# Two of the eight weight chunks of each gate and up product: the low part by an accumulating transfer in place of a VectorE subtraction

## The chip, the cores and the metric

The kernel runs on one core of one Trainium2 chip. Its engines are TensorE (PE: matrix products into PSUM; PEld is its weight load), VectorE (DVE), ScalarE (ACT), GpSimd (POOL) and SyncE (SP, which here issues the weight transfers). Each runs its own instructions in order and waits on semaphores for the others. The metric is the time of the program on the device in microseconds; a median of three runs is shown.

## What is computed

The reference is one layer of a decoder for 256 tokens of 2048 features: a combined input projection, sliding-window attention and a Mamba-2 mixer side by side, a gated merge, a feed-forward part, a per-layer embedding and a final norm. The part that matters here:

```
f = rmsnorm(h, g_ffn[i])                                            # h: 256 x 2048
h = h + (jax.nn.silu(f @ w_gate[i]) * (f @ w_up[i])) @ w_down[i]    # w_gate, w_up: 2048 x 5632
```

All weights and activations are float32.

## The kernel before

Each product is made of three TensorE products of rounded operands. A float32 matrix is split into a high part (the value rounded to float32r, a type that TensorE takes at full pace) and a low part (what the rounding left), and a product is hi*hi + hi*lo + lo*hi, summed in PSUM. The activations lie transposed in SBUF, split once (`hT` for the feed-forward part). The weights are streamed and split as they come.

`nblock` makes one block of 512 output columns. It goes through the 2048 input features in chunks of `kc` = 2 tiles of 128, so in eight chunks. For a chunk, SP's queue loads the weights, 128 partitions x 2 x 512 float32 or 512 KB, into `wr` (L181); ScalarE writes the high part `wh` (L188); VectorE writes the low part `wl` = `wr` - `wh` (L190). Then TensorE runs twelve matmuls: for each of the two feature tiles and the two token tiles one of L199 (`wh` under the high activations), one of L200 (`wl` under the high activations), and one of L201 (`wh` under the low activations). The first matmul of a chunk needs only `wh`; the second already needs `wl`.

The buffers come from pools that go round: four slots for `wr`, four for `wh`, three for `wl`. So `wl` of a chunk goes into the slot of the chunk three before, and its writer must wait until TensorE has read that one. The order of instructions on each engine is fixed when the program is built; semaphores do the rest.

The feed-forward part is in `hidden` (L834). For each of eleven column blocks j it calls `nblock` for the gate, then for the up product. The gate goes through ScalarE's Silu (L838), the two are multiplied on VectorE (L842), and the transposes of the result (L145) are put between the first chunks of the next gate block by `pump`. The blocks come in two halves, j = 0 to 5 and 6 to 10, each followed by the down product (L866). That is 22 gate and up blocks, 176 chunks. In this part GpSimd has next to nothing to do: it computes r3 at the start, and issues the transfers of `pt` and `gfin` (L861, L864) in the second half.

Of the kernel before, what the change touches and what calls it, by code (L numbers as in the profile page):

```python
# [18 lines left out]
P = 128  # L19
# [4 lines left out]
NB = 512  # L24
# [37 lines left out]
def block_kernel(ctx: ExitStack, tc: tile.TileContext, x, x_t, p_t, positions, vecs, rows, g_final,  # L62
# [25 lines left out]

    # work that runs beside the streaming products, a step per weight chunk from each queue
    side, heads = deque(), deque()  # L90
# [14 lines left out]

# [1 line left out]
    ident = const.tile([P, P], F32, name="ident")  # L107
# [6 lines left out]

# [1 line left out]
    def bcast_mid(ap, n):  # L116
# [7 lines left out]
    def split_to(dst, j0, ps, gains=None):  # L124
        """ps [128, 2, 256]: two transposed feature tiles, into the hi and lo parts of dst."""
        if gains is None:
            nc.scalar.copy(out=dst[:, 0, j0:j0 + 2, :], in_=ps)
            nc.vector.tensor_tensor(out=dst[:, 1, j0:j0 + 2, :], in0=ps,
                                    in1=dst[:, 0, j0:j0 + 2, :].bitcast(F32), op=ALU.subtract)
        else:  # L130
            for j in range(2):
                nc.scalar.activation(out=dst[:, 0, j0 + j, :], in_=ps[:, j, :], func=AF.Copy,
                                     scale=gains[j])
                nc.vector.scalar_tensor_tensor(out=dst[:, 1, j0 + j, :], in0=ps[:, j, :],  # L134
                                               scalar=gains[j],
                                               in1=dst[:, 0, j0 + j, :].bitcast(F32),
                                               op0=ALU.mult, op1=ALU.subtract)

    def transpose_pair(src, col0, dst, j0, gains=None):
        """Columns col0..col0+255 of the two token tiles, transposed, into dst[:, :, j0:j0+2]."""  # L140
        ps = aux_tile().rearrange("p (j t) -> p j t", j=2)
        for j in range(2):
            for t in range(NT):
                c = col0 + j * P
                nc.tensor.transpose(out=ps[:, j, t * P:(t + 1) * P], in_=src[t][:, c:c + P],  # L145
                                    identity=ident)
        split_to(dst, j0, ps, gains)
# [7 lines left out]
    def mean_parts(n, eps, name):  # L155
        """Partial means of squares per token tile, and eps beside them."""
        m = const.tile([P, NT, n + 1], F32, name=name)
        nc.vector.memset(m[:, :, n:n + 1], eps)
        return m
# [4 lines left out]
    def rsqrt_mean(parts, out_r):  # L164
        """parts [128, n, m] of mean_parts -> out_r [128, n]."""
        n = out_r.shape[1]
        s = stat_p.tile([P, NT], F32, name="rms_s")[:, :n]
        nc.vector.tensor_reduce(out=s, in_=parts, op=ALU.add, axis=AX.X)  # L168
        nc.gpsimd.tensor_tensor(out=out_r, in0=s, in1=mhalf[:, :n], op=ALU.pow)  # L169

    def nblock(w, col0, lhs, nk, subs=((0, NB),), pumps=1, before=None, kc=2):
        """Columns of w against transposed activations: hi*hi + hi*lo + lo*hi.

        Returns, per sub-block of columns, the two token tiles in PSUM."""
        width = sum(s[1] for s in subs)
        accs = [[acc_tile() for _ in range(NT)] for _ in subs]
        for c in range(nk // kc):
            if before is not None:
                before(c)
            wr = wraw_p.tile([P, kc, width], F32, name="wr", tag="wr")  # L180
            nc.sync.dma_start(  # L181
                out=wr, in_=w[c * kc * P:(c + 1) * kc * P, col0:col0 + width].rearrange(
                    "(k p) n -> p k n", p=P))
            wh = whi_p.tile([P, kc, width], F32R, name="wh", tag="wh")
# [4 lines left out]
            wl = wlo_p.tile([P, kc, width], F32R, name="wl", tag="wl")  # L189
            nc.vector.tensor_tensor(out=wl, in0=wr, in1=wh.bitcast(F32), op=ALU.subtract)  # L190
            for kk in range(kc):
# [13 lines left out]

# [1 line left out]
    warm = roll("warm")  # L207
# [14 lines left out]

    # 1 where column >= row; 1 where row > column
    upper = const.tile([P, P], F32, name="upper")
# [8 lines left out]
    nc.vector.tensor_copy(out=below_r, in_=below)  # L233
    # additive window mask over the previous and the own key block
    amask = const.tile([P, 2 * P], F32, name="amask")
# [27 lines left out]

    # pairs of feature tiles, ahead of the weights that meet them
    split_at = {0: 0, 1: 1, 3: 2, 5: 3, 7: 4, 9: 5, 10: 6, 11: 7}
# [24 lines left out]

# [1 line left out]
    def evac_rows(ps, width, col0, dst, r):  # L292
# [4 lines left out]
    def conv_pair(src, col0, ctile, acc):  # L297
        """Two channel tiles: transpose, causal depthwise convolution; into acc [128, 2, 256]."""
        ps = aux_tile().rearrange("p (j t) -> p j t", j=2)
# [37 lines left out]

    # B block, with the transposes of x ahead of the chunks that need them
    accs = nblock(w_in, BO, lhs_u, KD, pumps=0, before=load_u, kc=1)
# [3 lines left out]

    # angles of the rotary embedding, reduced to [-pi, pi]
    rot = const.tile([P, NT, 2, HD // 2], F32, name="rot")

    def make_rot():
        pos_f = stat_p.tile([P, NT], F32, name="pos_f")
        nc.vector.tensor_copy(out=pos_f, in_=pos_i)
        # the angle of |position|; the sine takes the sign back  # L350
        sgn = stat_p.tile([P, NT], F32, name="pos_sgn")
# [32 lines left out]
        for c in (c1, c2, c3, c4):  # L384
            less(k, c)
        # cosine as the sine a quarter turn on
        nc.vector.tensor_scalar(out=kh, in0=ang, scalar1=float(np.pi / 2), scalar2=None,
# [16 lines left out]

    # C block and dt
    W2 = (NB + SSM_H) // 2
# [20 lines left out]
    def make_dt():  # L427
# [5 lines left out]
        nc.scalar.activation(out=e, in_=e, func=AF.Exp)  # L433
        # log(1 + e) = 2 atanh(e / (2 + e))
        s = t3("dt_s")
# [39 lines left out]
    def queue_decay(g):  # L475
        """Decay matrices of group g, one token chunk after the other, times C B^T."""
        builds, products = [], []
# [112 lines left out]

# [1 line left out]
    # heads h and h + 4 of each eight side by side, as their key heads lie in kT  # L592
    qrot = big([P, NT, NH, HD], F32, name="qrot")
    kk = big([P, 2, NKV * SEQ], F32, name="kk")
    krot = kk[:, 0, :NT * NKV * HD].rearrange("p (t h d) -> p t h d", t=NT, h=NKV)
    kT = kk[:, 1].rearrange("p (h k) -> p h k", h=NKV)
    # values beside zeros, left for the even and right for the odd head of a feature tile
    vz = [big([P, NT, NKV, 2, 2, HD], F32R, name="vz") for _ in range(2)]
# [4 lines left out]
    def rope(ps, t, dst):  # L603
        """Four heads in PSUM columns; dst [128, 4, 64]."""
        pv = ps.rearrange("p (h a d) -> p h a d", h=4, a=2)
# [56 lines left out]
    def queue_heads(g):  # L662
# [46 lines left out]
        def p_flip():  # L709
            s = mix.pop(("s", g))  # L710
            # [keys, parity, pair, queries]: both query blocks on the first keys, one on the others
            pt = [big([P, 2, 2, 3 * P], F32R, name="pt") for _ in range(2)]
# [47 lines left out]

# [1 line left out]
    merged = [big([P, D], F32, name="merged") for _ in range(NT)]  # L762
# [45 lines left out]

# [1 line left out]
    h = [big([P, D], F32, name="h") for _ in range(NT)]  # L810
# [21 lines left out]

# [1 line left out]
    def hidden(j, dst):  # L834
        accs = nblock(w_gate, j * NB, lambda k: stat(hT, k), KD)
        act = [roll("act") for _ in range(NT)]
        for t in range(NT):
            nc.scalar.activation(out=act[t], in_=accs[0][t], func=AF.Silu,  # L838
                                 scale=r3[:, t:t + 1])
        accs = nblock(w_up, j * NB, lambda k: stat(hT, k), KD)  # L840
        for t in range(NT):
            nc.vector.scalar_tensor_tensor(out=act[t], in0=accs[0][t], scalar=r3[:, t:t + 1],  # L842
                                           in1=act[t], op0=ALU.mult, op1=ALU.mult)
        for i in range(2):
            side.append(lambda i=i: transpose_pair(act, i * 2 * P, dst, 2 * i))
# [31 lines left out]

# [1 line left out]
    ssq5 = mean_parts(5, EPS, "ssq5")  # L879
# [4 lines left out]
    def load_last(c):  # L884
        """Weights of the last block of columns, kept whole so that one token tile can end
        before the other."""
        wr = wraw_p.tile([P, 2, NB], F32, name="wr", tag="wr")
# [7 lines left out]
    def mix_in(t, ps, pp, c0, n):  # L895
        """h += sigmoid(gate) * proj on n columns from c0."""
        gt = roll("gt")[:, :n]
        hc = h[t][:, c0:c0 + n]
        nc.scalar.activation(out=gt, in_=ps, func=AF.Sigmoid, scale=r4[:, t:t + 1])
        nc.vector.tensor_tensor(out=gt, in0=gt, in1=pp, op=ALU.mult)  # L900
        nc.vector.tensor_tensor(out=hc, in0=hc, in1=gt, op=ALU.add)
# [120 lines left out]
```

## Time and profile before

| | |
|---|---|
| Median of 3 runs | 1625.88 us (1624.92 to 1626.29) |
| Span of the profiled execution | 1623.2 us |
| TensorE busy | 1600.3 us, 99% |
| VectorE busy | 915.8 us, 56% |
| ScalarE busy | 775.8 us, 48% |
| GpSimd busy | 142.1 us, 9% |
| Weight queue of SP | 290.75 MB, 58.6% of the 16 DMA engines |
| GpSimd's transfers | 3.47 MB, 0.6% |

The span is the time from the first to the last instruction of the one execution that was profiled, which is all that is known of that execution's own time; it is 2.7 us under the median of the runs. TensorE's matmuls are pipelined, and a matmul's length in the rows (0.39 us) overlaps with the next: the distance between two starts (0.23 us) is its cost.

### The profile page before, as it was taken

The numbers are of one execution on the slowest core, as the hardware profiler recorded it, in microseconds if no ns is written. First come the engines' busy times: TensorE is split into PE (matmuls) and PEld (weight loads), VectorE is DVE, ScalarE is ACT, GpSimd is POOL, SyncE is SP. The second block draws the span as 40 slices with busy tenths as digits, with TensorE's granted clock in tenths as the row PEclk, the third lists the DMA queues.
The fourth block names the chain that finished last, engine by engine and source line by source line (L and its number), as shares of the span: only waits on it lengthen the run. The fifth ranks groups of instructions, "written<-read, shape, count | busy, mean of one in ns | idle before, by whom it ended". The sixth has DMA issues, their size and how long they took to land.

```text
span 1623.2 us, 19872 instructions
## 1 busy us (share of the span) xinstructions
PE 1600.3 (99%) x7414; PEld 1326.0 (82%) x7414; DVE 915.8 (56%) x1062; ACT 775.8 (48%) x991; POOL 142.1 (9%) x144
## 2 busy tenths in 40 slices
PE   8999999999999999999999999999999999999997
PEld 6888888888888888888888888888888888888876
DVE  8777576665655555555555545444545454555673
ACT  6545665465543444445544444433344444454552
POOL 5023233313100000000000000000000000000000
PEclk9999999999999999999999999999999999999999
DMA  6765445555556666555666666556666676555671
GB/s 201 212 185 165 131 118 160 149 171 171 164 199 220 190 188 190 182 194 184 192 186 190 189 187 192 186 194 193 194 195 187 189 223 187 193 183 190 198 233 52
DMA packets 152433, 296.63 MB, mean 183 GB/s; under 512 B 9408, under 2 KB 9536, under 8 KB 151952
## 3 DMA queue, kind: packets, MB, share of 16 engines
q1 hardware_dynamic: 151040, 290.75, 58.6%
q0 software_dynamic: 576, 3.47, 0.6%
q8 instruction: 58, 0.95, 0.2%
q10 hardware_dynamic: 720, 1.14, 0.2%
q14 instruction: 39, 0.32, 0.1%
HBM read 293.23 MB, written 2.10 MB: 182 GB/s over the span
## 4 chain that ended last, share of the span: by engine, by line
PE 93%; DVE 2%; ACT 2%; DMA 1%; issue 1%; POOL 0%; POOLq 0%; ACTq 0%
PE acc L200 29%; PE acc L199 29%; PE acc L201 29%; PE aux L145 1%; DVE wl L190 1%; ACT sc L698 1%; PE aux L557 1%; DMA wr<-in_w_ple_gate_dram 1%; PE aux L734 1%; PE aux L496 0%; DMA wr<-in_w_in_dram 0%; ACT wh L188 0%; PE aux L303 0%; PE aux L718 0%; DVE uT L134 0%
## 5 line engine op out<-in xcount | busy, mean ns | idle before, releaser
L190 DVE TENSOR_TENSOR wl<-wr,wh 128x1024 fp32r<-128x1024 f32 (+2 forms) x556 | 687.0, 1239 | 568.6 <-PE acc L200 511.8
L188 ACT CAST wh<-wr 128x1024 fp32r<-128x1024 f32 (+2 forms) x555 | 570.6, 1030 | 710.8 <-PE acc L201 667.2
L199 PE MATMUL acc<-wh,uT 128*128 128x512 f32 (+1 forms) x704 | 277.0, 394 | 2.6 <-ACT cb L294 1.5
L200 PE MATMUL acc<-wl,uT 128*128 128x512 f32 (+1 forms) x704 | 270.4, 384 | 6.1 <-DVE wl L190 6.0
L199 PE MATMUL acc<-wh,hT 128*128 128x512 f32 x704 | 275.7, 392 | 0.0
L201 PE MATMUL acc<-wh,hT 128*128 128x512 f32 x704 | 274.2, 390 | 0.0
L200 PE MATMUL acc<-wl,hT 128*128 128x512 f32 x704 | 274.0, 389 | 0.0
L201 PE MATMUL acc<-wh,uT 128*128 128x512 f32 (+1 forms) x704 | 269.4, 383 | 0.0
L200 PEld LDWEIGHTS acc<-wl,uT 128*128 128x128 f32 x704 | 132.8, 189 | 35.4 <-DVE wl L190 10.8
L199 PEld LDWEIGHTS acc<-wh,uT 128*128 128x128 f32 x704 | 132.6, 189 | 28.2 <-ACT cb L294 1.7
L201 PEld LDWEIGHTS acc<-wh,hT 128*128 128x128 f32 x704 | 132.1, 188 | 27.7
L200 PEld LDWEIGHTS acc<-wl,hT 128*128 128x128 f32 x704 | 132.2, 188 | 26.9
L199 PEld LDWEIGHTS acc<-wh,hT 128*128 128x128 f32 x704 | 132.2, 188 | 26.8
L201 PEld LDWEIGHTS acc<-wh,uT 128*128 128x128 f32 x704 | 132.5, 188 | 25.3
L199 PE MATMUL acc<-wh,actT 128*128 128x512 f32 x352 | 137.6, 391 | 0.0
L201 PE MATMUL acc<-wh,actT 128*128 128x512 f32 x352 | 137.2, 390 | 0.0
L200 PE MATMUL acc<-wl,actT 128*128 128x512 f32 x352 | 137.2, 390 | 0.0
L201 PEld LDWEIGHTS acc<-wh,actT 128*128 128x128 f32 x352 | 66.1, 188 | 13.7
L199 PEld LDWEIGHTS acc<-wh,actT 128*128 128x128 f32 x352 | 66.1, 188 | 13.5
L200 PEld LDWEIGHTS acc<-wl,actT 128*128 128x128 f32 x352 | 66.1, 188 | 13.4
L169 POOL TENSOR_TENSOR r<-rms_s,mhalf 128x2 f32<-128x2 f32 (+1 forms) x6 | 4.4, 740 | 583.7 <-DVE rms_s L168 583.7
L199 PE MATMUL acc<-wh,mergedT 128*128 128x512 f32 x128 | 50.5, 394 | 0.0
(271 smaller groups left out, 1613.8 us busy)
## 6 DMA issues: line engine op xcount, KB each, us to landing
wr<-in_w_in_dram SPq DMA_DIRECT2D x152, 512.0 KB, 3.7
wr<-in_w_gate_dram SPq DMA_DIRECT2D x88, 512.0 KB, 3.7
wr<-in_w_up_dram SPq DMA_DIRECT2D x88, 512.0 KB, 3.7
wr<-in_w_down_dram SPq DMA_DIRECT2D x88, 512.0 KB, 3.6
wr<-in_w_ssd_br_dram SPq DMA_DIRECT2D x32, 512.0 KB, 4.2
wr<-in_w_o_dram SPq DMA_DIRECT2D x32, 512.0 KB, 4.3
wr<-in_w_ple_gate_dram SPq DMA_DIRECT2D x32, 512.0 KB, 4.6
wr<-in_w_attn_br_dram SPq DMA_DIRECT2D x16, 512.0 KB, 4.5
```

Source lines behind the costliest of these rows:

```text
L145: nc.tensor.transpose(out=ps[:, j, t * P:(t + 1) * P], in_=src[t][:, c:c + P], identity=ident)
L169: nc.gpsimd.tensor_tensor(out=out_r, in0=s, in1=mhalf[:, :n], op=ALU.pow)
L188: nc.scalar.copy(out=wh, in_=wr)
L190: nc.vector.tensor_tensor(out=wl, in0=wr, in1=wh.bitcast(F32), op=ALU.subtract)
L199: nc.tensor.matmul(o, hi[:, ts], wh[:, kk, cs], start=(k == 0), stop=False)
L200: nc.tensor.matmul(o, hi[:, ts], wl[:, kk, cs], start=False, stop=False)
L201: nc.tensor.matmul(o, lo[:, ts], wh[:, kk, cs], start=False, stop=(k == nk - 1))
L557: nc.tensor.matmul(ps[:, es], m[:, t, e, :], xd[:, t, 0, es], start=True, stop=True)
L698: nc.scalar.activation(out=s[:, h, ks], in_=s[:, h, ks], func=AF.Exp, bias=mx[:, t, h:h + 1], accum_out=den[:, t, h:h + 1])
L734: nc.tensor.matmul(ps[:, :, qs], vz[vi][:, kt, g, a].rearrange("p b d -> p (b d)"), pt[pi][:, a, :, cs], start=(kt == 0 and a == 0 and vi ...
```

## The change

In `nblock` the chunks whose numbers are in `added` get their low part in another way: ScalarE writes the negated, rounded weights into `wl`, and then a transfer issued from GpSimd's queue reads the same weights once more from HBM and adds them to what lies in `wl`. The sum is `wl` = w - round(w), as before. `hidden` passes `added=(3, 7)` for both products, so it is 2 of 8 chunks, 44 in all. The other products keep the subtraction. Removed comments and docstrings are left out of the diff here; they move the line numbers by up to six (L200 becomes L206).

```diff
-    def nblock(w, col0, lhs, nk, subs=((0, NB),), pumps=1, before=None, kc=2):
+    def nblock(w, col0, lhs, nk, subs=((0, NB),), pumps=1, before=None, kc=2,
+               added=()):
...
             wr = wraw_p.tile([P, kc, width], F32, name="wr", tag="wr")
-            nc.sync.dma_start(
-                out=wr, in_=w[c * kc * P:(c + 1) * kc * P, col0:col0 + width].rearrange(
-                    "(k p) n -> p k n", p=P))
+            wd = w[c * kc * P:(c + 1) * kc * P, col0:col0 + width].rearrange(
+                "(k p) n -> p k n", p=P)
+            nc.sync.dma_start(out=wr, in_=wd)
...
             wl = wlo_p.tile([P, kc, width], F32R, name="wl", tag="wl")
-            nc.vector.tensor_tensor(out=wl, in0=wr, in1=wh.bitcast(F32), op=ALU.subtract)
+            if c in added:
+                nc.scalar.activation(out=wl, in_=wr, func=AF.Copy, scale=-1.0)
+                nc.gpsimd.dma_start(out=wl, in_=wd, accum_op=ALU.add)
+            else:
+                nc.vector.tensor_tensor(out=wl, in0=wr, in1=wh.bitcast(F32), op=ALU.subtract)
...
-        accs = nblock(w_gate, j * NB, lambda k: stat(hT, k), KD)
+        accs = nblock(w_gate, j * NB, lambda k: stat(hT, k), KD, added=(3, 7))
...
-        accs = nblock(w_up, j * NB, lambda k: stat(hT, k), KD)
+        accs = nblock(w_up, j * NB, lambda k: stat(hT, k), KD, added=(3, 7))
```

What this does to the order on the engines is seen at the second gate block (j = 1). On ScalarE before, from the two Silu of the first gate (`act`) to the copies of the second block; the first five `wh` are chunks 3 to 7 of the up block, the next those of the gate block of j = 1 from its chunk 0, with `wh_6715` as chunk 3:

```order
L838 ACTIVATE act_6491<-acc_6345,r3_6337 128x512
L188 CAST wh_6552<-wr_6550 128x1024
L188 CAST wh_6570<-wr_6568 128x1024
L188 CAST wh_6588<-wr_6586 128x1024
L188 CAST wh_6606<-wr_6604 128x1024
L188 CAST wh_6624<-wr_6622 128x1024
L188 CAST wh_6647<-wr_6645 128x1024
L188 CAST wh_6672<-wr_6670 128x1024
L188 CAST wh_6697<-wr_6695 128x1024
L188 CAST wh_6715<-wr_6713 128x1024
L188 CAST wh_6733<-wr_6731 128x1024
L127 CAST actT_6343<-aux_6663 128x512
```

The end of the same stretch now, from chunk 7 of the up block (`wh_6627`) on; `wh_6719` is chunk 3 of the gate block:

```order
L190 CAST wh_6627<-wr_6625 128x1024
L193 ACTIVATE wl_6629<-wr_6625 128x1024
L190 CAST wh_6651<-wr_6649 128x1024
L190 CAST wh_6676<-wr_6674 128x1024
L190 CAST wh_6701<-wr_6699 128x1024
L190 CAST wh_6719<-wr_6717 128x1024
L193 ACTIVATE wl_6721<-wr_6717 128x1024
L127 CAST actT_6343<-aux_6667 128x512
L190 CAST wh_6738<-wr_6736 128x1024
```

The negating copy (L193) stands right behind its chunk's `wh` and ahead of the `wh` of the next chunk; the copy of the transposes (L127) has come ahead of chunk 4's `wh`.

On TensorE the matmuls stand in the same order as before; only what they wait for has changed. Before, at chunk 3 of that gate block, with the semaphore that each waits for:

```order
L201 MATMUL acc_6644<-wh_6697,hT_5652 128x512
L199 MATMUL acc_6643<-wh_6715,hT_5652 128x512 [waits Activation_49]
L200 MATMUL acc_6643<-wl_6717,hT_5652 128x512 [waits DVE_49]
L201 MATMUL acc_6643<-wh_6715,hT_5652 128x512
L199 MATMUL acc_6644<-wh_6715,hT_5652 128x512
L200 MATMUL acc_6644<-wl_6717,hT_5652 128x512
```

Now, at the same place:

```order
L207 MATMUL acc_6647<-wh_6701,hT_5652 128x512
L205 MATMUL acc_6648<-wh_6701,hT_5652 128x512
L206 MATMUL acc_6648<-wl_6703,hT_5652 128x512
L207 MATMUL acc_6648<-wh_6701,hT_5652 128x512
L205 MATMUL acc_6647<-wh_6719,hT_5652 128x512 [waits Activation_49]
L206 MATMUL acc_6647<-wl_6721,hT_5652 128x512 [waits DMASW0_49]
```

The second matmul of the chunk waited for VectorE and now waits for a transfer of GpSimd's queue (DMASW).

On GpSimd's queue nothing stood between `r3` and `pt` before. The end of the stage now, from the last gate block on:

```order
L194 DMA wl_10454<-in_w_gate_dram 128x2x512
L194 DMA wl_10527<-in_w_gate_dram 128x2x512
L867 DMA pt_10715<-in_p_t_dram 128x512
L194 DMA wl_10606<-in_w_up_dram 128x2x512
L194 DMA wl_10679<-in_w_up_dram 128x2x512
L870 DMA gfin_10719<-in_g_final_dram 128x2048
```

The 44 transfers (L194) stand one behind the other, and `pt` and `gfin` among the last of them.

## Rows read from the trace of the kernel before

**Rows 1.** The page's first part: span, then busy us, share, instructions

```profile
span 1623.2 us, 19872 instructions
...
PE 1600.3 (99%) x7414; PEld 1326.0 (82%) x7414; DVE 915.8 (56%) x1062; ACT 775.8 (48%) x991; POOL 142.1 (9%) x144
```

**Rows 2.** The page's slices: granted TensorE clock in tenths

```profile
PEclk9999999999999999999999999999999999999999
```

**Rows 3.** The page's costliest groups: busy us, mean ns, idle before and releaser

```profile
L190 DVE TENSOR_TENSOR wl<-wr,wh 128x1024 fp32r<-128x1024 f32 (+2 forms) x556 | 687.0, 1239 | 568.6 <-PE acc L200 511.8
...
L200 PE MATMUL acc<-wl,uT 128*128 128x512 f32 (+1 forms) x704 | 270.4, 384 | 6.1 <-DVE wl L190 6.0
```

**Rows 4.** Stretches: length; busy of PE, PEld, DVE, ACT, POOL; clock, DMA, GB/s

```profile
776.00:1045.00 269.00, 269.00 (x1215) 222.60 (x1214) 136.24 (x126) 118.95 (x129) 0.71 (x1) 1.00 0.65 190
...
1176.00:1396.00 220.00, 220.00 (x988) 182.12 (x987) 108.67 (x97) 93.50 (x97) 1.10 (x2) 1.00 0.66 196
```

**Rows 5.** Groups by line, 776 to 1396 us: busy us, mean ns, idle before

```profile
L190 DVE TENSOR_TENSOR wl<-wr,wh 128x1024 fp32r<-128x1024 f32 x224 | 274.3, 1224 | 284.6 <-PE acc L200 271.7 <-issue 9.2 <-ACT act L838 1.9
...
L188 ACT CAST wh<-wr 128x1024 fp32r<-128x1024 f32 x224 | 236.2, 1055 | 344.3 <-PE acc L201 341.2 <-DMA wr<-in_w_up_dram 1.9 <-issue 1.2
```

**Rows 6.** Timeline, 829.3 to 836 us: start, length, instruction, idle before it

```profile
829.34 0.39 PE L200 MATMUL acc<-wl,hT 128*128 128x512 f32 x1
...
829.76 1.23 DVE L190 TENSOR_TENSOR wl<-wr,wh 128x1024 fp32r<-128x1024 f32 x1 [0.69 <-PE acc L200]
...
829.99 1.06 ACT L188 CAST wh<-wr 128x1024 fp32r<-128x1024 f32 x1 [1.64 <-PE acc L201]
...
831.05 3.11 SPq L181 DMA_DIRECT2D wr<-in_w_up_dram  x2
...
835.23 0.39 PE L199 MATMUL acc<-wh,hT 128*128 128x512 f32 x1
...
835.46 0.39 PE L200 MATMUL acc<-wl,hT 128*128 128x512 f32 x1
```

**Rows 7.** Timeline of a gate block's start, 822.9 to 830.1 us

```profile
823.42 1.23 DVE L190 TENSOR_TENSOR wl<-wr,wh 128x1024 fp32r<-128x1024 f32 x1 [0.62 <-issue]
...
826.61 0.60 PE L145 MATMUL aux<-ident,act 128*128 128x128 f32 x4
...
830.02 0.39 PE L200 MATMUL acc<-wl,hT 128*128 128x512 f32 x1
```

**Rows 8.** DMA issues: out<-in, queue, count, KB each, median us to landing

```profile
wr<-in_w_gate_dram SPq DMA_DIRECT2D x88, 512.0 KB, 3.7
...
gfin<-in_g_final_dram POOLq DMA_DIRECT2D x1, 1024.0 KB, 7.5
...
pt<-in_p_t_dram POOLq DMA_DIRECT2D x1, 256.0 KB, 5.3
...
pos_i<-in_positions_dram POOLq DMA_DIRECT2D x1, 1.0 KB, 3.7
```

**Rows 9.** Line L812, the two h transfers: issues in ns, times to landing

```profile
L812 POOL DMA_DIRECT2D h<-in_x_dram x2: 530/568/605, 457.3 to 503.3; - x2
...
DMA to landing us min/median/max: 5.9/6.6/7.2
```

**Rows 10.** Timeline of TensorE, 1562 to 1572 us

```profile
1566.51 0.50 PE L199 MATMUL acc<-wh,h2T 128*128 128x512 f32 x1 [3.45 <-ACT gt L899]
...
1568.46 0.63 PE L199 MATMUL acc<-wh,h2T 128*128 128x512 f32 x1
1568.89 0.63 PE L200 MATMUL acc<-wl,h2T 128*128 128x512 f32 x1
...
1571.42 0.39 PE L200 MATMUL acc<-wl,h2T 128*128 128x512 f32 x1
```

**Rows 11.** Timeline of TensorE, 24 to 29 us

```profile
28.31 0.61 PE L200 MATMUL acc<-wl,uT 128*128 128x512 f32 x1 [2.33 <-DVE wl L190]
```

**Rows 12.** Stretch of 28 to 30 us, columns as in rows 4

```profile
28.00:30.00 2.00, 1.69 (x5) 1.30 (x5) 2.00 (x6) 0.00 (x0) 0.85 (x1) 0.64 0.31 70
```

## The prediction

> **What bounds the kernel now.** I read the page from the top: the span and the engines' shares, then the slices, then the costliest groups with the idle time ahead of them, and last the stage that is changed. TensorE is busy for 99% of 1623.2 us, VectorE for 56%, ScalarE for 48%, GpSimd for 9% [rows 1], at the full granted clock in every slice [rows 2]. The reader should see who waits for whom. In the whole kernel VectorE sits idle 568.6 us ahead of `wl` (L190), and 511.8 of that ends at a matmul of L200, the reader of `wl`. The other way round, the group of L200 that waits at all waited 6.0 us for `wl` [rows 3]. The producer waits for the consumer: a slot of `wl` must come free before the next is written.
>
> The change lies in the feed-forward stage. Its gate and up blocks fill 776 to 1045 us and 1176 to 1396 us, 489 us, and there TensorE is busy without a gap, at clock 1.00, with a DMA share of 0.65 to 0.66 [rows 4]. From 776 to 1396 us the subtractions waited 271.7 us for TensorE, and ScalarE's copies 341.2 us for TensorE and 1.9 us for a transfer [rows 5]. So the stage goes at TensorE's pace, and taking work from VectorE wins nothing. What counts is whether `wl` is still in time.
>
> **How much time a chunk's `wl` has.** `wl` of chunk c can be begun when TensorE has read that of c-3, and is wanted by the second matmul of c. In the timeline the last L200 of a chunk begins at 829.34 us and lasts 0.39, VectorE starts the next `wl` at 829.76, and the chunk three on has its first matmuls at 835.23 and 835.46 [rows 6]. That is 835.46 - 829.76 = 5.70 us. The subtraction takes 1.23 us; 4.47 us are spare. Nine of the gate blocks (all but the first of each half) have two groups of transposes between their chunks 0 and 3. There VectorE starts at 823.42, and the chunk three on has its L200 at 830.02: 6.60 us [rows 7].
>
> **The change, part by part.**
>
> *Removed:* 44 subtractions of 1224 ns [rows 5] on an engine that waits. They give 0 on the path.
>
> *Added on ScalarE:* 44 negating copies of 128x1024. The copy of the same shape takes 1055 ns there [rows 5]. As load that is 44 x 1.06 = 47 us, hidden in the 344.3 us of idle time ahead of L188 in the stage [rows 5]. The negating copy must wait for the slot of c-3, and `wh` of c+1 stands behind it; it starts some 1.1 us later and is wanted only two chunks on. Without that cover it would cost up to 1.06 us a time. In the chain of its own chunk the 1.06 us count in full, from the moment when the subtraction would have started.
>
> *Added on GpSimd's queue:* the accumulating transfer, which waits for the negating copy. GpSimd has nothing else in the stage but r3, `pt` and `gfin`; an issue took 0.53 to 0.61 us on it [rows 9], and the transfers come eleven us apart, four chunks, so none is held up by another.
>
> *Moved:* from free slot to matmul the chain was one subtraction; now it is copy, hand-over, transfer, hand-over. I put the two hand-overs at 0.1 us (VectorE starts 0.03 us after the end of the matmul that frees its slot [rows 6]). With L from issue to landing, TensorE stands 1.06 + 0.1 + L - 5.70, about L - 4.5 us, at each of 35 chunks, and L - 5.4 at nine. The stalls add up: `wl` of c+4 can't be begun before TensorE is through c+1, so no stall pays for the next.
>
> *L* is the disputed price; the trace has no accumulating transfer. GpSimd's plain ones beside this weight stream landed in 3.7 us (1 KB), 5.3 (256 KB) and 7.5 (1024 KB, behind another) [rows 8]; the two `h` transfers of 1024 KB in 5.9 and 7.2 [rows 9]. The chunk is 512 KB. Half of what the slower `h` takes beyond the smallest, 3.7 + (7.2 - 3.7) / 2 = 5.45, is my estimate of a plain copy, and the lower bound. An accumulating transfer reads its destination as well as its source, 1024 KB in all. That makes `h` the nearest row; I take 7.2 rather than 5.9, since this transfer has rows of 2 KB where `h` has 8 KB, and so more pieces. If the bytes cost twice what they cost in `h`, L is 3.7 + 2 x 3.5 = 10.7; half of that excess, 9.0, bounds the range.
>
> The stall is then 7.2 - 4.5 = 2.7 us at 35 chunks and 1.8 at nine: 94.5 + 16.2 = **111 us**. On the profiled execution's 1623.2 us that gives 1734; the median of the runs shown, 1625.88, is 2.7 above its span, so the forecast is **1737 us**, 6.8% slower.
>
> *The weight stream* gets company. The stage's share of 0.65 over 489 us is 318 us of the DMA engines for 176 chunks, 1.8 a chunk; 44 more at twice that are 159 us, and (318 + 159) / (489 + 111) = 0.80: not full. A weight chunk issued at 831.05 [rows 6] lands 3.7 us later [rows 8], at 834.8; its `wh` copy comes three chunks (8.2 us) after that of 829.99 [rows 6], at 838.2. With 3.4 us of cover I put this at 0; without it, each us of delay would count 44 times.
>
> The Trainium skill gives a rule to hold against these rows: "DMA: Bandwidth & Descriptors", section "Anatomy of one DMA — SWDGE (gpsimd) path", fits a GpSimd transfer as 2.0 us and its bytes at 436 GB/s. By that, as an estimate, 512 KB would take 3.2 us and 1024 KB 4.4, and no chunk would stall: the sum would be 0. The trace's own 1024 KB took 5.9 to 7.5 us, so it does not agree beside this stream, and the sum goes by the rows.
>
> **The rivals.**
>
> *The transfer is hidden anyway (not slower).* Place: the first L200 of each such chunk. It decides at L = 4.5 us. For it: the smallest GpSimd transfer landed in 3.7 us, and SP's own 512 KB chunks in 3.7 [rows 8]; if accumulating costs no more than a plain copy of SP, all is in time and the result is 1626 us. Against: 256 KB from GpSimd already took 5.3. By the skill's rule above this is what happens. Chance 0.12, a part of it at small losses (at L = 5.0, 35 x 0.5 = 18 us).
>
> *The stalls also cost clock.* A TensorE wait of 3.45 us was followed, some two us later, by matmuls 0.43 us apart (1568.46, 1568.89) instead of 0.23 [rows 6], up to 1571.42 us: seven of them, 7 x 0.2 = 1.4 us lost [rows 10]. A wait of 2.33 us, after thin work, ended at 28.31 us [rows 11], in a stretch with a mean clock of 0.64 [rows 12]. If each of 44 stalls did so it would cost 44 x 1.4 = 62 us more, 1799 us; half of them, 1768. Against: 2.7 is below 3.45, and TensorE works without a gap for some eleven us between stalls. Chance 0.17.
>
> *Accumulating is much slower than reading.* L of 9.0 gives stalls of 4.5 and 3.6 us: 158 + 32 = 190, 1816 us. L of 10.7 gives 6.2 and 5.3: 265, 1891 us, clock not counted. For it: no row shows the price of the addition. Against: it moves no more bytes than I counted. Chance 0.12.
>
> *A gain* would need TensorE's pace to depend on VectorE's traffic, and no row shows that. Chance 0.02.
>
> *The change doesn't do what it says:* the built program has 44 subtractions fewer, 44 transfers more, and a matmul waiting for each; I give this nothing.
>
> **How the numbers follow.** The forecast, stalls of 1 to 3.5 us with few falls of the clock, has 0.57; its own range is 1665 to 1780. For 8 in 10 the range leaves out the hidden transfer below and the slowest accumulations above: from 1655 (L = 5.45 with stalls of 0.95 us at 35 chunks, 33 us, 1659) to 1840. A measurement of this kernel tells 0.2%, 3 us, from no change. Same has 0.09 (the hidden case without its small losses), faster 0.02, slower 0.89.
>
> **What would show it.** Right: TensorE's busy share in the stage falls to about 489 / 600 = 82%, with 44 waits at the old L200 put down to the transfer, 2.7 us each and 0.9 less at nine; `wl` lands about 7 us after its issue; the negating copy takes 1.06 us and begins when the slot is freed; other stages keep their times to 1 us. Wrong: landing under 4.5 us and no waits; landing near 10; a granted clock below 0.95 in the stage; or waits at the first matmul of a chunk, since then the weight stream or `wh` is late, which I put at nothing.

## The result and the profile after

The changed kernel takes 1834.05 us (median of 4 runs, 1832.13 to 1836.95) against 1626.09 us before: a ratio of 1.1283 with a 95% interval of 1.127 to 1.1296, 208 us more. The forecast was 1737 us with a range of 1655 to 1840: the right side, inside the range by 6 us, and 97 us short. The ratios here and below leave out a run more than 1.5% above the fastest of the same kernel; there is one, the run of 1715.79 us with the late `wl` matmuls.

The page's first part, slices and queue of GpSimd, to be held against [rows 1, 2]:

```profile
span 1830.4 us, 19912 instructions
...
PE 1670.3 (91%) x7414; PEld 1365.4 (75%) x7414; DVE 862.7 (47%) x1018; ACT 816.3 (45%) x1035; POOL 197.1 (11%) x188
...
PEclk9999999999999999999989998999988998899999
...
q0 software_dynamic: 12544, 26.54, 8.1%
```

TensorE no longer fills the span, and the clock row, all nines before, has eights in the slices of the gate and up blocks. The stretches say where the time lies (columns as in [rows 4]: gate and up of the first half, its down blocks, gate and up of the second, its down blocks):

```profile
776.00:1155.00 379.00, 304.63 (x1204) 241.03 (x1202) 105.64 (x101) 140.00 (x151) 29.66 (x25) 0.91 0.62 168
1155.00:1286.00 131.00, 131.00 (x583) 108.52 (x582) 64.59 (x59) 51.78 (x50) 0.00 (x0) 1.00 0.59 189
1286.00:1598.00 312.00, 251.23 (x988) 199.01 (x987) 85.61 (x78) 113.12 (x118) 25.29 (x22) 0.90 0.64 173
1598.00:1711.00 113.00, 113.00 (x509) 93.43 (x508) 60.28 (x63) 51.83 (x66) 0.00 (x0) 0.99 0.56 182
```

The first and third grew from 269 + 220 = 489 us [rows 4] to 379 + 312 = 691: 202 us of the 207 by which the span grew. The down blocks keep their pace. Two things changed in the stretches: TensorE stands idle, and its clock is 0.91 and 0.90 instead of 1.00.

TensorE's waits from 776 to 1598 us (total, times, longest):

```profile
PE acc L206 <- DMA wl<-in_w_up_dram: 73.3, 22, 4.2
PE acc L206 <- DMA wl<-in_w_gate_dram: 61.9, 22, 3.8
```

The same view of the trace before has none in this stage. They are 44, all at the matmul that needs `wl`, and come to 135.2 us, 3.07 each. One of them in the timeline, an up block's chunk 3:

```profile
811.30 0.39 PE L206 MATMUL acc<-wl,hT 128*128 128x512 f32 x1
...
811.72 1.06 ACT L193 ACTIVATE wl<-wr 128x1024 fp32r<-128x1024 f32 x1 [0.38 <-PE acc L206]
...
813.08 1.20 POOL L194 DMA_DIRECT2D wl<-in_w_up_dram  x1 [15.08 <-ACT wl L193]
...
817.19 0.39 PE L205 MATMUL acc<-wh,hT 128*128 128x512 f32 x1
...
820.80 0.50 PE L206 MATMUL acc<-wl,hT 128*128 128x512 f32 x1 [3.23 <-DMA wl<-in_w_up_dram]
821.14 0.40 PE L207 MATMUL acc<-wh,hT 128*128 128x512 f32 x1
821.38 0.40 PE L205 MATMUL acc<-wh,hT 128*128 128x512 f32 x1
```

Read it as the chain of the prediction. The slot is freed at 811.69, the negating copy begins at 811.72 and ends at 812.78, GpSimd issues at 813.08, and the second matmul of the chunk, due 0.23 us after the first at 817.42, begins at 820.80. The issues and their landing:

```profile
wl<-in_w_gate_dram POOLq DMA_DIRECT2D x22, 512.0 KB, 7.6
wl<-in_w_up_dram POOLq DMA_DIRECT2D x22, 512.0 KB, 7.8
```

A pause costs a little more than its wait. A matmul's row is 0.39 us long where its pace is 0.23, so 0.16 us of each pause don't show as idle, and after a pause the next two steps are 0.34 and 0.24 us instead of 0.23: together about 0.3 us, 13 us over 44.

And some pauses are followed by matmuls at half clock. The one above is not; the next, of 3.53 us, is:

```profile
835.55 0.50 PE L206 MATMUL acc<-wl,hT 128*128 128x512 f32 x1 [3.53 <-DMA wl<-in_w_up_dram]
...
836.67 0.63 PE L207 MATMUL acc<-wh,hT 128*128 128x512 f32 x1
837.09 0.63 PE L205 MATMUL acc<-wh,hT 128*128 128x512 f32 x1
...
839.65 0.51 PE L205 MATMUL acc<-wh,hT 128*128 128x512 f32 x1
```

Here the starts lie 0.43 us apart instead of 0.23. In the timeline of the stage 30 of the 44 pauses are followed like this, 21 of them by six to eight such matmuls and nine by 11 to 13.

### The profile page after: what moved, and what is told of

Read it like the earlier page. It is cut to its first block, busy times and chain, and to the rows that moved or that the text cites. A ratio compares the mean times of both kernels' runs of the same rounds, so it can differ in the third digit from the quotient of the medians.

```text
span 1830.4 us, 19912 instructions
## 1 busy us (share of the span) xinstructions
PE 1670.3 (91%) x7414; PEld 1365.4 (75%) x7414; DVE 862.7 (47%) x1018; ACT 816.3 (45%) x1035; POOL 197.1 (11%) x188
## 4 chain that ended last, share of the span: by engine, by line
PE 50%; issue 40%; DMA 3%; POOL 3%; ACT 2%; DVE 2%; POOLq 0%; ACTq 0%; DVEq 0%
PE acc L206 15%; PE acc L205 15%; PE acc L207 15%; POOL wl L194 3%; DMA wl<-in_w_up_dram 1%; PE aux L145 1%; DMA wl<-in_w_gate_dram 1%; ACT sc L704 1%; PE aux L563 1%; DVE wl L196 1%; DMA wr<-in_w_ple_gate_dram 1%; DMA wr<-in_w_in_dram 1%; PE aux L740 0%; PE aux L502 0%; PE aux L309 0%
## 5 line engine op out<-in xcount | busy, mean ns | idle before, releaser
L196 DVE TENSOR_TENSOR wl<-wr,wh 128x1024 fp32r<-128x1024 f32 (+2 forms) x512 | 633.4, 1240 | 753.2 <-PE acc L206 701.1
L206 PE MATMUL acc<-wl,hT 128*128 128x512 f32 x704 | 303.4, 431 | 135.1 <-DMA wl<-in_w_up_dram 73.3
L207 PE MATMUL acc<-wh,hT 128*128 128x512 f32 x704 | 296.9, 422 | 0.0
L205 PE MATMUL acc<-wh,hT 128*128 128x512 f32 x704 | 296.9, 422 | 0.0
L206 PEld LDWEIGHTS acc<-wl,hT 128*128 128x128 f32 x704 | 146.2, 208 | 184.5 <-DMA wl<-in_w_up_dram 82.6
L206 PE MATMUL acc<-wl,uT 128*128 128x512 f32 (+1 forms) x704 | 270.2, 384 | 5.4 <-DVE wl L196 5.4
L205 PEld LDWEIGHTS acc<-wh,hT 128*128 128x128 f32 x704 | 145.4, 207 | 32.9
L207 PEld LDWEIGHTS acc<-wh,hT 128*128 128x128 f32 x704 | 146.3, 208 | 31.1
L206 PEld LDWEIGHTS acc<-wl,uT 128*128 128x128 f32 x704 | 132.9, 189 | 33.2 <-DVE wl L196 8.4
L206 PE MATMUL acc<-wl,actT 128*128 128x512 f32 x352 | 137.1, 390 | 0.0
L206 PEld LDWEIGHTS acc<-wl,actT 128*128 128x128 f32 x352 | 66.2, 188 | 13.6
L194 POOL DMA_DIRECT2D wl<-in_w_gate_dram x22 | 26.6, 1208 | 438.1 <-ACT wl L193 438.1
L193 ACT ACTIVATE wl<-wr 128x1024 fp32r<-128x1024 f32 x44 | 46.7, 1061 | 60.7 <-PE acc L206 60.7
```

Source lines behind the costliest of these rows:

```text
L193: nc.scalar.activation(out=wl, in_=wr, func=AF.Copy, scale=-1.0)
L194: nc.gpsimd.dma_start(out=wl, in_=wd, accum_op=ALU.add)
L205: nc.tensor.matmul(o, hi[:, ts], wh[:, kk, cs], start=(k == 0), stop=False)
L206: nc.tensor.matmul(o, hi[:, ts], wl[:, kk, cs], start=False, stop=False)
L207: nc.tensor.matmul(o, lo[:, ts], wh[:, kk, cs], start=False, stop=(k == nk - 1))
```

## The experiments

Each was made from the changed kernel, and timed against the kernel before on the same chip (medians there 1625.2 and 1625.3 us). The theory ("A"): `wl` is late, TensorE waits, and the waits lower the clock. The rivals: the cost is the added traffic, GpSimd's issue path, or ScalarE's extra copies.

**The transfer without the addition.**

```diff
-                nc.gpsimd.dma_start(out=wl, in_=wd, accum_op=ALU.add)
+                nc.gpsimd.dma_start(out=wl, in_=wd)
```

> The transfer of GpSimd's queue only writes the weights over wl and adds nothing, so the low part is wrong data of the same size (the addition is left out); everything else stands as in the changed kernel. If the price of L lies in the second reading and the adding (theory A, my prediction's step), the landing falls from 7.7 us to about 5.5, the waits from 3.1 us to about 1, few falls of the clock remain, and the time is about 1660 to 1685 us. If it lies in GpSimd's issue path and the queue (rival B), the landing stays at 7 us or more and the time within 20 us of 1834.

Measured: 1660.68 us, ratio 1.0219 (1.0197 to 1.024). GpSimd's issues and their landing:

```profile
L194 POOL DMA_DIRECT2D wl<-in_w_up_dram x22: 698/713/716, 803.8 to 1422.5; - x22
...
DMA to landing us min/median/max: 4.4/4.9/7.8
```

The same bytes from the same queue land in 4.9 us instead of 7.7 (the median of all 44) when nothing is added, and the issue takes 0.71 us instead of 1.20. TensorE's waits come to 20.3 us. So 2.8 us of each landing are the price of accumulating (the longer issue may be 0.5 of them), and without them four fifths of the loss are gone: 35 us remain of 208.

**VectorE adds in place of the transfer.**

```diff
-                nc.gpsimd.dma_start(out=wl, in_=wd, accum_op=ALU.add)
+                nc.vector.tensor_tensor(out=wl, in0=wr, in1=wl.bitcast(F32), op=ALU.add)
```

> ScalarE's negating copy stays, and VectorE adds the raw weights to it in place of the transfer; the result is the same low part. Theory A: the chain is 1.06 + 1.23 us of the 5.7 us that a chunk has, nothing waits, the time is 1626 us within 0.2%, and so ScalarE's 44 copies cost nothing. Rival B: if the copies hold up the wh copies behind them, TensorE waits at the first matmul of a chunk and the time is 1640 us or more.

Measured: 1624.4 us, ratio 1.0004 (0.9994 to 1.0014), no wait of TensorE in the stage. ScalarE's 44 copies are free, as the prediction had it.

**Work for TensorE in its pauses.**

```diff
+FILL = 12
...
+            if c in added:
+                fill = aux_tile()
+                for i in range(FILL):
+                    nc.tensor.matmul(fill, lhs(kc * c)[0][:, 0:P], wh[:, 0], start=True, stop=True)
             for kk in range(kc):
```

> Twelve matmuls of 128x512 more, into a PSUM tile that nobody reads, ahead of each of the 44 chunks: 12 x 0.227 = 2.7 us of work where TensorE waited 3.1 us. Theory A (about 65 us of the loss is half clock after the waits): the granted clock of the stage goes back to 0.99 or more, a wait of some 0.5 us remains, and the time falls to about 1770 to 1785 us although work is added. Rival B (matmuls are slow because of the added traffic, or the clock falls whatever TensorE does): the clock stays at about 0.96 and the time stays at 1834 us or rises.

Measured: 1772.16 us, ratio 1.0902 (1.0886 to 1.0918): 528 matmuls more, and 62 us less than the changed kernel. The two stretches, and the waits that are left:

```profile
776.00:1126.00 350.00, 339.40 (x1494) 274.01 (x1493) 105.32 (x100) 140.53 (x151) 29.66 (x25) 1.00 0.66 182
1256.00:1541.00 285.00, 279.62 (x1230) 226.60 (x1229) 85.71 (x79) 113.75 (x119) 25.29 (x22) 1.00 0.68 187
```

```profile
PE acc L211 <- DMA wl<-in_w_up_dram: 10.0, 18, 1.6
PE acc L211 <- DMA wl<-in_w_gate_dram: 5.9, 13, 1.1
```

The clock is back at 1.00 with the transfers as slow as they were (7.7 and 7.5 us). So the slow matmuls came from the idle pauses, not from the traffic. The work put in (528 x 0.227 = 120 us) and the waits that are left (16 us) are together as long as the 135 us of waits before; the 62 us are what the clock had cost.

**The matmuls of `wl` last.** In the 44 chunks the order becomes eight matmuls with `wh`, then four with `wl`:

```diff
+            if c in added:
+                steps.sort(key=lambda s: s[3] == 1)
...
```

> In the 44 chunks the eight matmuls that need only wh come first, and the four that need wl last, so wl is wanted 7 x 0.227 = 1.6 us later. Theory A: the waits fall from 3.1 to about 1.5 us (66 us in all), the clock falls seldom, and the time is about 1690 to 1710 us. Rival B (the waits are a matter of throughput, and what is won at one chunk is lost at the next): the time falls by less than 40 us.

Measured: 1705.21 us (median of four, 1690.23 to 1715.79), ratio of the other three 1.0462 (1.0414 to 1.0511). Landing is unchanged (7.6 us), the waits:

```profile
PE acc L207 <- DMA wl<-in_w_up_dram: 32.8, 22, 2.5
PE acc L207 <- DMA wl<-in_w_gate_dram: 28.3, 22, 2.2
```

That is 61.1 us, 1.39 each where there were 3.07: 1.7 less for 1.6 us of later need. The clock in the two stretches is 0.99, and four of the 44 pauses are followed by half clock. Taking 74 us from the waits took about 129 from the time (118 to 144 by the single runs), since the clock came with them.

**Chunk 7 alone**, `added=(7,)` in both products.

> Only chunk 7 of each block has its low part by the transfer, 22 in place of 44. Theory A: each stall stands by itself, so 22 waits of 3.2 us (chunk 7 has no transposes ahead of it) and about as many falls of the clock as half of the stalls had, 22 x 3.2 + 32 = 102 us: about 1715 to 1735 us. Rival B (neighbouring stalls feed each other, or the pauses must come close together to cost clock): 1700 us or less.

Measured: 1727.72 us, ratio 1.0625 (1.0606 to 1.0645).

```profile
PE acc L206 <- DMA wl<-in_w_up_dram: 33.9, 11, 4.1
PE acc L206 <- DMA wl<-in_w_gate_dram: 33.8, 11, 3.8
```

```profile
776.00:1100.00 324.00, 286.80 (x1196) 231.56 (x1196) 118.70 (x111) 127.75 (x139) 15.22 (x13) 0.94 0.60 176
1230.00:1499.00 269.00, 238.46 (x1000) 192.65 (x998) 98.86 (x90) 103.92 (x109) 13.21 (x12) 0.95 0.62 182
```

Half the stalls, 3.08 us each, and half the loss (102 of 208 us). If a share 2 x (1 - clock) of a stretch is at half clock, and half of that is lost, the loss is (1 - clock) x length: 0.06 x 324 + 0.05 x 269 = 33 us, with 67.7 us of waits. Each stall stands by itself, and pauses with 22 us of work and more between them cost clock too: 18 of the 22 are followed by slow matmuls.

**Begun earlier.** The chunk's `wl` gets a buffer of its own, and the negating copy and the transfer stand ahead of the `wh` copy:

```diff
+            if c in added:
+                wl = big([P, kc, width], F32R, name="wl")
+                nc.scalar.activation(out=wl, in_=wr, func=AF.Copy, scale=-1.0)
+                nc.gpsimd.dma_start(out=wl, in_=wd, accum_op=ALU.add)
...
                 nc.scalar.copy(out=wh, in_=wr)
```

> The same 44 accumulating transfers, but their wl lies in a buffer of its own (of the pool big, which has room in this stage), and the negating copy stands ahead of the chunk's wh copy on ScalarE, so that it need not wait for the slot of chunk c-3. In the order of the program this brings the copy about two chunks forward at 35 chunks; at the nine gate blocks with transposes the copy of chunk 3 stands behind wh of chunk 4 and a copy of the transposes, some 1.6 us later than before. Theory A (lateness): no waits at the 35, about 4 us at the nine, 36 us, and some 10 us of clock: 1660 to 1685 us. Rival B (the added traffic of the 44 transfers itself slows the stream or TensorE): waits or slow matmuls at the 35 too, and 1720 us or more.

Measured: 1694.72 us, ratio 1.0424 (1.0408 to 1.044). This was 10 us over the expected range, but all but one of the waits lie where they were expected:

```profile
PE acc L207 <- DMA wl<-in_w_gate_dram: 46.1, 10, 5.9
```

The 22 up chunks, begun early, never waited; of the gate's 22 ten did, 4.6 us each: chunk 3 of the nine blocks with transposes, and of the first block. The clock is 0.95 in both stretches, (299 + 260) x 0.05 = 28 us where 10 were expected. The landing has a part in the longer waits:

```profile
wl<-in_w_gate_dram POOLq DMA_DIRECT2D x22, 512.0 KB, 8.3
wl<-in_w_up_dram POOLq DMA_DIRECT2D x22, 512.0 KB, 6.0
```

In these ten gate blocks the transfers of chunk 3 and chunk 7 are issued 4.5 to 5.1 us apart and are under way together.

**The same with chunk 3 of the gate left to VectorE**, 33 transfers.

> As the run with early copies, but chunk 3 of the gate blocks keeps the subtraction: 33 accumulating transfers, all of them begun early. Theory A: nothing waits, the clock stays at 1.00, and the time is that of the kernel before, 1626 us within 0.2%; the taken subtractions give nothing back, since VectorE waits for TensorE anyway. Rival B: 33/44 of a cost that belongs to the traffic remains, 1640 us or more.

Measured: 1632.13 us, ratio 1.0038 (1.0025 to 1.005). No matmul waited for a transfer. The two stretches and the landing:

```profile
776.00:1047.00 271.00, 267.89 (x1206) 221.45 (x1206) 113.24 (x107) 134.91 (x146) 22.44 (x19) 1.00 0.77 223
1178.00:1400.00 222.00, 222.00 (x996) 183.79 (x995) 89.99 (x82) 106.09 (x112) 19.26 (x17) 1.00 0.77 226
```

```profile
wl<-in_w_up_dram POOLq DMA_DIRECT2D x22, 512.0 KB, 6.0
wl<-in_w_gate_dram POOLq DMA_DIRECT2D x11, 512.0 KB, 5.9
```

The DMA engines are busy for 0.77 of the time instead of 0.65, and TensorE keeps its pace. The expected "within 0.2%" was missed by a little: 6.9 us remain, and two waits of 6.4 us in all by transposes behind VectorE's multiplication are in this trace and not in that of the kernel before:

```profile
PE aux L145 <- DVE act L849: 6.4, 2, 3.3
```

At the first of them (3.1 us, followed by seven slow matmuls) ScalarE had waited 6.3 us for a weight chunk of the down product. The seven chunks that SP issued from 1025 to 1046 us landed late:

```profile
DMA to landing us min/median/max: 3.5/8.9/10.1
```

The late chunk was issued at 1032.7 us, 1.9 us after an accumulating transfer, and two more followed it within 1.6 us. So rival B is not wholly out: a little of these 6.9 us may belong to the traffic, which was not tried by itself.

**Half of the bytes.** Only the second feature tile's half of `wl` goes by copy and transfer; VectorE subtracts the first.

```diff
+                nc.scalar.activation(out=wl[:, 1], in_=wr[:, 1], func=AF.Copy, scale=-1.0)
+                nc.gpsimd.dma_start(out=wl[:, 1], in_=wd[:, 1], accum_op=ALU.add)
+                nc.vector.tensor_tensor(out=wl[:, 0], in0=wr[:, 0], in1=wh[:, 0].bitcast(F32),
+                                        op=ALU.subtract)
...
```

> In the 44 chunks only the second feature tile's half of wl (256 KB) is made by negating copy and transfer; the first half is subtracted on VectorE. It is wanted six matmuls later, 5.70 + 6 x 0.227 = 7.06 us after the slot is free, and the copy takes half as long. Theory A (L is 3.7 us and a part in proportion to the bytes, 3.7 + 4.0 / 2 = 5.7): 0.56 + 0.1 + 5.7 = 6.4, in time, so 1626 us with at most some 15 us of small waits. Rival B (L is mostly fixed, 7 us for half the bytes too): 0.6 us of wait at each, 1650 us or more.

Measured: 1628.22 us, ratio 1.0014 (1.0005 to 1.0024).

```profile
PE acc L208 <- DMA wl<-in_w_up_dram: 1.3, 3, 0.9
PE acc L208 <- DMA wl<-in_w_gate_dram: 0.7, 1, 0.7
```

All 44 chunks still use the transfer, and it lands in 5.5 us (median of the 44; 5.0 to 7.1), wanted 1.4 us later: four small waits are left. No run of this series beats the kernel before, which is what a waiting VectorE lets one expect.

## Why the prediction was right, and where it was short

**What bounds the kernel, and that nothing is won on VectorE:** right. With 44 additions on VectorE the time is that of before to within 0.1%. Where the transfers come in time and VectorE has less to do (33 chunks, or half of 44), it is 0.4 and 0.1% longer, not shorter.

**The chain and its time limit:** right. The limit of 5.70 us holds in the trace after: the slot was freed at 811.69 us, and `wl` was due at 817.42. The waits are 44, at the matmul named, each for itself (chunk 7 alone has the same 3.08 us), and a later need, half the bytes or an earlier start shorten or remove them as the difference L - 4.5 says. The nine gate chunks behind transposes waited 2.3 us and the other 35 3.3 us, on average in the timeline: 0.9 less at the nine, as forecast.

**The size of the wait:** 111 us forecast, 135 measured, 148 with the 13 us that a pause costs beside its wait. Two terms were too small. L was put at 7.2 us and is 7.7; the hand-overs at 0.1 us, where GpSimd alone began 0.30 us after the end of the copy (812.78 to 813.08). With these two put right the sum gives 1.06 + 0.30 + 7.7 - 5.70 = 3.36 us at 35 chunks and 2.46 at nine, 140 us; measured are 135 us and 7 us that don't show as idle (44 x 0.16). The other 6 of the 13 us, the slower steps after a pause, had no term. The working behind L had a wrong part in it: a plain copy lands in 4.9 us, below the 5.45 that was taken for the lower bound, and accumulating adds 2.8, not the 1.75 that a second reading of the same bytes would have cost by [rows 8, 9].

**"Few falls of the clock":** this is the step that failed. The sum had 0 for it, and the rival "the stalls also cost clock" had a chance of 0.17 and a price of 62 us. It came true, and near that price: filling the pauses gave 62 us back, and (1 - clock) x length gives 0.09 x 379 + 0.10 x 312 = 65 us. That the price fits is in part luck: it was 1.4 us at each of 44 stalls, and 30 were followed by half clock, nine of them by nearly twice the seven matmuls that the price was made of. The prediction had named a granted clock below 0.95 as a sign that it was wrong, and the clock is 0.91 and 0.90. One argument against the rival, that 2.7 us is below the one wait of 3.45 us that had been followed by a half clock [rows 10], had weighed a single case as if it were a bound: a pause of 2.09 us is among the 30. The wait of 2.33 us [rows 11, 12], put aside because thin work stood ahead of it, was the better guide. The other argument, that TensorE works without a gap for some eleven us between stalls, fell with chunk 7 alone, where 22 us of work lie between.

Together: 135 of waits, 13 beside them, 62 to 65 of clock, 210 to 213 against 208 measured. The upper end of the range was not made for these two errors together: the clock rival by itself came to 1799 us, an L of 9.0 us to 1816. That 1834 us still lies 6 us under it is luck too.

**The covers:** the weight stream and `wh` were put at 0, and are: TensorE waited for neither in the stage. SP's chunks of the gate landed later than before (4.6 us against 3.7 [rows 8]) within their cover of 3.4 us, and in the run with 33 transfers, with the DMA engines at 0.77, TensorE waited in the two stretches only once, for 3.1 us.

**The rival "hidden anyway"** needed L of 4.5 us, and fell. The rule of the Trainium skill behind it, "DMA: Bandwidth & Descriptors", section "Anatomy of one DMA — SWDGE (gpsimd) path", gives 3.2 us for 512 KB, as an estimate. A plain one took 4.9 here and an accumulating one 7.7, so the trace does not agree with it for either.

## What to carry to other kernels

Moving work from an engine that waits to a transfer won nothing here, and the transfer then stood in a chain with a fixed limit: measure from the moment when the buffer comes free to the first reader, and compare that with copy, hand-over, issue and landing before anything else. A stall on TensorE has to be costed twice, the wait and the half clock that can follow; a wait of 3.07 us here cost 4.7 on average, one of 1.39 us about 1.8. If such a transfer must be used, give it a buffer of its own and start it a chunk or two earlier (with the 33 that could be started so, 7 us of loss were left), or let it carry half the bytes (3 us were left). A reader that comes last was not enough by itself: 80 us were left.

## What the runs showed of the hardware

An accumulating transfer of 512 KB from HBM to SBUF on GpSimd's queue took 7.7 us from issue to landing, the plain one 4.9, and GpSimd was busy 1.20 us instead of 0.71 with its issue. The same transfer landed in 6.0 us (5.5 to 8.7) in the run with 33 transfers. How close it follows a weight transfer of SP seems to matter. In the changed kernel all 44 were issued within 0.7 us after one (as at 813.08, after SP's at 812.81) and landed in 6.8 to 8.7 us. In the run with 33, the six that were issued within 0.7 us after one landed in 6.4 to 8.5 us, and the ten issued 3 us or more after one in 5.5 to 6.1. That the company on the DMA engines is the reason is argued; no run varied it alone.

The clock fell after pauses shorter than the 3.45 us of [rows 10]: with 22 waits of 3.08 us it was at 0.94 to 0.95, with 44 waits of 3.07 us at 0.90 to 0.91, with 44 of 1.39 us at 0.99, and with the pauses filled at 1.00. No single length parts the pauses that cost clock from those that don't. In the changed kernel one of 2.09 us was followed by half clock, and one of 3.49 us was not, up to the next pause:

```profile
913.49 0.50 PE L206 MATMUL acc<-wl,hT 128*128 128x512 f32 x1 [2.09 <-DMA wl<-in_w_gate_dram]
...
915.39 0.63 PE L207 MATMUL acc<-wh,hT 128*128 128x512 f32 x1
915.82 0.63 PE L205 MATMUL acc<-wh,hT 128*128 128x512 f32 x1
...
1056.71 0.50 PE L206 MATMUL acc<-wl,hT 128*128 128x512 f32 x1 [3.49 <-DMA wl<-in_w_gate_dram]
...
1058.89 0.39 PE L206 MATMUL acc<-wl,hT 128*128 128x512 f32 x1
1059.12 0.39 PE L207 MATMUL acc<-wh,hT 128*128 128x512 f32 x1
```

In the run with the late `wl` matmuls the four that were followed by half clock were of 1.80 to 2.09 us, while one of 2.48 us was not. What decides it at a single pause stays open.
